# Tile offsets, the order of the up products, and GpSimd's share in a float32r transformer block

## The chip, the core and the metric

The kernel runs on one core of a Trainium2 chip. The metric is the time of one execution on the device, in microseconds, as the median of several runs. The core has TensorE (PE, matmuls), VectorE (DVE), ScalarE (ACT), GpSimd (POOL), a queue engine (SP) and 16 DMA engines. PE's clock has two levels, 1.2 and 2.4 GHz; "granted clock" 1.00 is 2.4 GHz.

## What is computed

One block of a diffusion transformer over 256 latent tokens and 256 context tokens of width 2048, all in float32: adaLN modulation, a mixing sub-layer with windowed attention and a pooling mixer, a squared-ReLU MLP, and a last RMSNorm.

```python
sh_a, sc_a, g_a, sh_m, sc_m, g_m = ada_modulation(c, w_ada, b_ada)      # silu(c) @ w_ada + b_ada, 2048 x 12288
h  = modulate(rms_norm(x, norm_attn_w), sh_a, sc_a)
q, k, v, u = split_projection(h @ w_in)                                 # 2048 x 2560, latent and context
attn = latent_window_attention(rope(q), rope(k), v, kc, vc, attn_sink)
pool = multiscale_pool(u, pool_w, pool_scale)
x  = x + g_a * (concat([attn, pool]) @ w_out)                           # 2048 x 2048
hm = modulate(rms_norm(x, norm_mlp_w), sh_m, sc_m)
x  = x + g_m * (square(relu(hm @ w_up)) @ w_down)                       # 2048 x 8192, 8192 x 2048
return rms_norm(x, final_norm_w)
```

## The kernel before

**Products.** A float32 product is made of float32r products: each operand is split into a high part (a cast on ACT) and a low part (a subtraction), and three matmuls are added in PSUM, high by high, high by low and low by high (`mm3`, lines 280 to 282). A matmul reads a stationary operand (128 columns, loaded by its own instruction, PEld in the profile) and a moving operand (256 or 512 columns).

**Weights.** `WeightStream` brings all weights in order, in tiles of 1 MB through five `raw` slots, on SP's queue. Each half of a weight tile is split by `split_to`: the cast to `hi` on ACT (line 89), the subtraction to `lo` (line 91) on DVE, or, for every third half among the first 140 tiles, on POOL. `hi` and `lo` have six slots each, and the splits run six halves ahead of their use. Tiles of w_ada are used unsplit, on PE (line 297) or, for some columns, on DVE as sums of scaled rows (`ada_v`, line 319).

**Stages.** (1) Up to about 200 us, normalization and the in-projection: `ps_k` and `ps_qu` take the weights as stationary and the activations `hhi`, `hlo` as moving operand, `ps_v` the other way round; w_ada for the attention is spread between them. (2) Attention to about 320 us. (3) The out-projection, `ps_w`: the tiles `mx` stationary, weights moving; after each group of 512 columns, DVE multiplies by the gate, POOL (DVE in the last group) adds the residual (line 817), ACT takes the squares. (4) The first three up groups with `mm3` and the rest of the late w_ada work, to about 525 us. (5) Then 13 up groups and 8 rounds of down products in turn. An up group (`up_group`) keeps four PSUM banks; for each weight tile it walks 4 banks by 4 rows of the tile and issues a wide matmul (`hi` with high and low activations side by side, 512 columns, line 876) and a narrow one (`lo` with the high activations, 256 columns, line 877) in turn. `activation` turns the four sums into `ahi` and `alo`. A down product (`down_group`) has `ahi` and `alo` stationary and the weights moving. The order of the instructions on each engine follows the code.

**Where tiles lie.** A pool puts its tags one after the other in the order in which they are first asked for, each with all its slots; pools on the left side grow upwards, each after the one that is open before it, and those on the right downwards. Every slice that a matmul takes of the tiles named below starts a multiple of 512 bytes into its tile, so the start of an operand modulo 512 is that of its tile. In the built program of the kernel before they start at these bytes of each partition (modulo 512 in brackets): `hi` 64672 (160), `lo` 89248 (160), all `mx` tiles (160), `hhi` and `hlo` in the pool hpa 187872 and 191968 (480), in hpb 130208 and 134304 (160), `ahi` 182048 (288), `alo` 194336 (288). The pool hpa serves the chunks 0, 1, 4 and 5 of the activations, hpb the chunks 2, 3, 6 and 7.

## Time and profile before

| | us |
|---|---|
| median of 3 runs (1172.6 to 1174.21) | 1173.42 |
| the profiled execution, its own time | 1171.78 |
| its span, first to last instruction | 1170.0 |
| PE busy | 1120.1 (96%) |
| DVE busy | 820.6 (70%) |
| ACT busy | 507.4 (43%) |
| POOL busy | 145.2 (12%) |
| mean granted clock | 0.983 |

"Busy" is the time in which an engine executes; matmuls are pipelined, so the time of one of them in a row (0.39 us for 512 columns) is longer than the step from its start to the next one's start. The pace of a product is the step between starts. A group of instructions is shown as line, engine, operation, output<-inputs, shapes and count, then busy time and mean ns of one, then idle time before them and what ended it. Times in a timeline count from the start of the span.

### The profile page before, as it was taken

To read this page: it belongs to the slowest core of one execution; us is meant where nothing else is said; L and a number is where in the kernel's file an instruction comes from. 1 tells how busy PE (TensorE), PEld (TensorE's weight loads), DVE (VectorE), ACT (ScalarE), POOL (GpSimd) and SP (SyncE) were. 2 spreads that over 40 slices of the span, in tenths; PEclk is the share of its full clock that TensorE was granted. 3 is DMA by queue.
4 is the path that set the end of the run, shared out by engine and by line. 5 is a ranking of instruction groups with operands and counts; after the bars stand their busy time and mean duration, and the time that the engine had idled before them with its cause. 6 is when DMAs were issued, how large, how long until landed. Compare 5 with 4: busy or idle time off the path is not lost.

```text
span 1170.0 us, 16111 instructions
## 1 busy us (share of the span) xinstructions
PE 1120.1 (96%) x6308; PEld 905.4 (77%) x6308; DVE 820.6 (70%) x1255; ACT 507.4 (43%) x760; POOL 145.2 (12%) x98
## 2 busy tenths in 40 slices
PE   3999999989999979899999999999999999999996
PEld 2767788746588859888888888888888888888884
DVE  5655467988698888897865775774664664676576
ACT  4633233377543433365433433443533543543452
POOL 1011124610143312330000000000000000000001
PEclk9999999989999979999999999999999999999998
DMA  9999898667898899968785685686556655565531
GB/s 342 331 335 330 287 333 272 224 233 264 272 327 279 294 328 316 329 241 287 254 274 187 232 276 180 235 287 197 181 181 186 200 189 180 190 199 187 180 108 72
DMA packets 174012, 286.64 MB, mean 245 GB/s; under 512 B 5609, under 2 KB 72353, under 8 KB 172785
## 3 DMA queue, kind: packets, MB, share of 16 engines
q1 hardware_dynamic: 172800, 279.55, 71.3%
q0 software_dynamic: 848, 5.55, 1.3%
q8 instruction: 49, 0.80, 0.3%
q10 hardware_dynamic: 288, 0.52, 0.1%
q14 instruction: 27, 0.21, 0.0%
HBM read 283.50 MB, written 2.10 MB: 244 GB/s over the span
## 4 chain that ended last, share of the span: by engine, by line
PE 81%; DVE 11%; DMA 3%; issue 2%; ACT 1%; SPq 1%; DVEq 0%; ACTq 0%
PE ps_up L876 17%; PE ps_d L281 10%; PE ps_d L282 10%; PE ps_d L280 10%; PE ps_up L877 8%; PE ps_ada L297 4%; DVE ada_v L319 3%; DVE lo L91 3%; PE ps_qu L280 2%; PE ps_qu L282 2%; PE ps_qu L281 2%; PE ps_o L725 2%; DMA raw<-in_w_in_dram 1%; PE tp_p L714 1%; PE ps_w L280 1%
## 5 line engine op out<-in xcount | busy, mean ns | idle before, releaser
L91 DVE TENSOR_TENSOR lo<-raw,hi 128x1024 fp32r<-128x1024 f32 x293 | 376.1, 1298 | 212.4 <-ACT hi L89 212.0
L89 ACT CAST hi<-raw 128x1024 fp32r<-128x1024 f32 x330 | 338.0, 1050 | 400.5 <-PE ps_d L282 157.3
L876 PE MATMUL ps_up<-mx,hi 128*128 128x512 f32 x832 | 293.3, 397 | 0.0
L877 PE MATMUL ps_up<-mx,lo 128*128 128x256 f32 x832 | 233.0, 280 | 0.0
L280 PE MATMUL ps_d<-hi,ahi 128*128 128x512 f32 x512 | 200.8, 395 | 0.0
L281 PE MATMUL ps_d<-lo,ahi 128*128 128x512 f32 x512 | 200.7, 395 | 0.0
L282 PE MATMUL ps_d<-hi,alo 128*128 128x512 f32 x512 | 197.8, 395 | 0.0
L876 PEld LDWEIGHTS ps_up<-mx,hi 128*128 128x128 f32 x832 | 156.1, 188 | 37.9 <-issue 1.0
L877 PEld LDWEIGHTS ps_up<-mx,lo 128*128 128x128 f32 x832 | 157.0, 189 | 1.1 <-issue 1.0
L91 POOL TENSOR_TENSOR lo<-raw,hi 128x1024 fp32r<-128x1024 f32 x37 | 95.3, 2577 | 333.1 <-ACT hi L89 304.2
L319 DVE SCALAR_TENSOR_TENSOR ada_v<-raw,c_sil,ada_v 128x512 f32<-128x512 f32 x135 | 124.4, 921 | 13.8 <-DMA raw<-in_w_ada_dram 12.0
L280 PEld LDWEIGHTS ps_d<-hi,ahi 128*128 128x128 f32 x512 | 96.4, 188 | 22.7
L282 PEld LDWEIGHTS ps_d<-hi,alo 128*128 128x128 f32 x512 | 96.4, 188 | 22.7
L281 PEld LDWEIGHTS ps_d<-lo,ahi 128*128 128x128 f32 x512 | 96.4, 188 | 22.4
L280 PE MATMUL ps_qu<-hhi,hi 128*128 128x256 f32 x256 | 75.2, 294 | 5.9 <-ACT hhi L447 5.9
L297 PE MATMUL ps_ada<-raw,c_sil 128*32 128x512 f32 x480 | 73.8, 626 | 0.2 <-DMA raw<-in_w_ada_dram 0.2
L281 PE MATMUL ps_qu<-hlo,hi 128*128 128x256 f32 x256 | 72.4, 284 | 0.0
L282 PE MATMUL ps_qu<-hhi,lo 128*128 128x256 f32 x256 | 71.8, 284 | 0.0
L957 POOL DMA_DIRECT2D fw<-in_final_norm_w_dram x1 | 0.6, 571 | 569.0 <-DVE lo L91 569.0
L280 PEld LDWEIGHTS ps_qu<-hhi,hi 128*128 128x128 f32 x256 | 49.0, 191 | 23.9 <-issue 11.9
L282 PE MATMUL ps_up<-mx,lo 128*128 128x256 f32 x192 | 53.1, 285 | 4.6 <-DVE lo L91 4.6
L281 PE MATMUL ps_up<-mx,hi 128*128 128x256 f32 x192 | 53.7, 283 | 0.0
(196 smaller groups left out, 1457.1 us busy)
## 6 DMA issues: line engine op xcount, KB each, us to landing
raw<-in_w_ada_dram SPq DMA_DIRECT2D x128, 512.0 KB, 7.3
raw<-in_w_mlp_up_dram SPq DMA_DIRECT2D x64, 1024.0 KB, 5.5
raw<-in_w_mlp_down_dram SPq DMA_DIRECT2D x64, 1024.0 KB, 5.1
raw<-in_w_ada_dram SPq DMA_DIRECT2D x32, 1024.0 KB, 6.6
raw<-in_w_in_dram SPq DMA_DIRECT2D x19, 1024.0 KB, 7.0
raw<-in_w_out_dram SPq DMA_DIRECT2D x16, 1024.0 KB, 6.7
xnat<-in_x_dram SPq DMA_DIRECT2D x2, 1024.0 KB, 6.0
xnat<-in_ctx_dram SPq DMA_DIRECT2D x2, 1024.0 KB, 11.8
```

The source lines that it names most:

```text
L89: nc.scalar.copy(hi, raw)
L91: eng.tensor_tensor(lo, raw, hi.bitcast(F32), ALU.subtract)
L280: nc.tensor.matmul(ps, a[0], b[0], start=first, stop=False, skip_group_check=True)
L281: nc.tensor.matmul(ps, a[0], b[1], start=False, stop=False, skip_group_check=True)
L282: nc.tensor.matmul(ps, a[1], b[0], start=False, stop=last, skip_group_check=True)
L297: nc.tensor.matmul(ps[32 * j : 32 * j + 32, :], c_sil[:, 4 * kg + j, :], raw[:, j, :], start=(kg == 0), stop=(kg == 3), tile_position=(0, ...
L319: nc.vector.scalar_tensor_tensor(box["e"], raw[:, j, :], sc, box["e"], ALU.mult, ALU.add)
L714: nc.tensor.transpose(tp[:, P * k : P * k + P], self.p[:, i, P * k : P * k + P], ident)
L725: nc.tensor.matmul(ps[64 * i : 64 * i + 64, 0:T], va[k // 2][:, k % 2, 64 * g : 64 * g + 64], pT[:, k, i, :], start=(k == 0), stop=(k == 3 ...
L876: nc.tensor.matmul(pss[m], hi, hm[k][2], start=k == 0, stop=False, skip_group_check=True)
L877: nc.tensor.matmul(pss[m][:, 0:T], lo, hm[k][0], start=False, stop=k == KC - 1, skip_group_check=True)
L957: nc.gpsimd.dma_start(out=fw, in_=final_w.partition_broadcast(P))
```

## The change

1. Gap tiles, which no instruction reads or writes, move the tiles behind them: 320 bytes between `hi` and `lo`, 192 at the start of mixa and of hpb, 320 between `hhi` and `hlo` (which are now two slots of one tag each), 320 at the end of hpa, 64 between `ahi` and `alo`. `rstd`'s scratch tiles of the last norm (192 bytes) go from the pool mp to yp. From the sizes the starts modulo 512 become:

| tile | before | after |
|---|---|---|
| `hi` | 160 | 160 |
| `lo` | 160 | 480 |
| `mx` | 160 | 160 |
| `hhi`, hpa / hpb | 480 / 160 | 352 / 352 |
| `hlo`, hpa / hpb | 480 / 160 | 160 / 160 |
| `ahi` | 288 | 416 |
| `alo` | 288 | 480 |

(`ahi`: the pool mp ends where x2 starts, at 212960, and holds 2048 + 12288 + 64 + 12288 + 2048 + 4096 bytes, so it starts at 180128 and `ahi` at 182176.) The tiles of the attention's scores do not move.

2. In `up_group` the 16 wide matmuls of a weight tile come first, then its 16 narrow ones.

3. POOL computes no lower parts and no residual additions: 37 subtractions of line 91 and six additions of line 817 go to DVE.

```diff
-POOL_SPLITS = 140
+def gap(pool, n, name="gap"):
+    pool.tile([P, n // 4], F32, tag=name, name=name, bufs=1)
@@ split_to
             hi = self.pool.tile([P, 2, 512], F32R, tag="hi", name="hi", bufs=N_HALF)
+            if not self.n_half:
+                gap(self.pool, 320)
             lo = self.pool.tile([P, 2, 512], F32R, tag="lo", name="lo", bufs=N_HALF)
             nc.scalar.copy(hi, raw)
-            eng = nc.gpsimd if i < POOL_SPLITS and self.n_half % 3 == 1 else nc.vector
-            eng.tensor_tensor(lo, raw, hi.bitcast(F32), ALU.subtract)
+            nc.vector.tensor_tensor(lo, raw, hi.bitcast(F32), ALU.subtract)
@@ modulated
-            hhi = pool.tile([P, 2, 512], F32R, tag=f"hhi{c_ % 2}", name="hhi", bufs=1)
-            hlo = pool.tile([P, 2, 512], F32R, tag=f"hlo{c_ % 2}", name="hlo", bufs=1)
+            hhi = pool.tile([P, 2, 512], F32R, tag="hhi", name="hhi", bufs=2)
+            if c_ in (0, 2):
+                gap(pool, 320, "gaph")
+            hlo = pool.tile([P, 2, 512], F32R, tag="hlo", name="hlo", bufs=2)
@@ where the pools are opened and closed
             mixa = ctx.enter_context(tc.tile_pool(name="mixa", bufs=1, side="left", reuse_waits="tile"))
+            gap(mixa, 192)
             hpb = hpb_es.enter_context(tc.tile_pool(name="hpb", bufs=1, side="left", reuse_waits="tile"))
+            gap(hpb, 192)
+    gap(hpa, 320)
     st_es.close()
     hpa_es.close()
@@ out_group
-            eng = nc.vector if dg == 3 else nc.gpsimd
-            eng.tensor_tensor(xs, xs, t, ALU.add)
+            nc.vector.tensor_tensor(xs, xs, t, ALU.add)
@@ activation
         ahi = mp.tile([P, 4, T], F32R, tag="ahi", name="ahi", bufs=3)
+        gap(mp, 64)
         alo = mp.tile([P, 4, T], F32R, tag="alo", name="alo", bufs=3)
@@ up_group
-            for m in range(4):
-                for j in range(4):
-                    k = 4 * kg + j
-                    hi, lo = w(j, slice(P * m, P * m + P))
-                    nc.tensor.matmul(pss[m], hi, hm[k][2], start=k == 0, stop=False, skip_group_check=True)
-                    nc.tensor.matmul(pss[m][:, 0:T], lo, hm[k][0], start=False, stop=k == KC - 1, skip_group_check=True)
+            for part in range(2):
+                for m in range(4):
+                    for j in range(4):
+                        k = 4 * kg + j
+                        wk = w(j, slice(P * m, P * m + P))[part]
+                        ps, h = (pss[m][:, 0:T], hm[k][0]) if part else (pss[m], hm[k][2])
+                        nc.tensor.matmul(ps, wk, h, start=part == k == 0, stop=part == 1 and k == KC - 1, skip_group_check=True)
@@ finish
-        r = rstd(mp, (ss3[:, i, 3:4], mean[:, i : i + 1]), 1)
+        r = rstd(yp, (ss3[:, i, 3:4], mean[:, i : i + 1]), 1)
```

## Rows read from the trace of the kernel before

**Rows 1.** Stretches: length, busy us of PE PEld DVE ACT POOL, clock, DMA share
```profile
60.00:190.00 130.00, 130.00 (x947) 99.25 (x945) 74.28 (x117) 40.12 (x49) 27.96 (x19) 1.00 0.95 317
190.00:320.00 130.00, 122.16 (x804) 79.25 (x802) 109.01 (x250) 75.97 (x175) 37.73 (x33) 0.96 0.72 248
320.00:390.00 70.00, 70.00 (x329) 57.36 (x328) 61.12 (x60) 27.53 (x35) 27.67 (x13) 1.00 0.91 312
390.00:493.00 103.00, 91.71 (x638) 81.27 (x636) 90.83 (x130) 39.42 (x56) 28.53 (x13) 0.93 0.92 310
493.00:1150.00 657.00, 656.89 (x3282) 551.19 (x3282) 439.87 (x554) 288.57 (x382) 11.81 (x5) 1.00 0.63 209
```

**Rows 2.** Chain of waits from 390 to 493 us, shares by line
```profile
by line: DVE ada_v L319 27.3%; DVE lo L91 20.2%; issue 15.9%; DMA raw<-in_w_out_dram 8.0%; DMA raw<-in_w_mlp_up_dram 5.7%; PE ps_up L282 3.9%; PE ps_up L280 3.4%; PE ps_up L281 3.4%; PE ps_adac L327 2.1%; ACT hi L89 2.1%; DVE mx L848 2.1%; 
```

**Rows 3.** Stretches, one product's matmuls alone: w_out, down, up (PE busy, matmuls)
```profile
329.93:351.27 21.34, 21.34 (x95) 1.00 0.93 314
1023.77:1068.15 44.38, 44.23 (x191) 1.00 0.59 191
979.39:1023.65 44.26, 44.12 (x255) 1.00 0.57 186
```

**Rows 4.** Timeline of PE, v product (start us, us, what); 14 matmuls between
```profile
145.29 0.28 PE L280 MATMUL ps_v<-hi,hhi 128*128 128x256 f32 x1
...
146.99 0.28 PE L280 MATMUL ps_v<-hi,hhi 128*128 128x256 f32 x1
```

**Rows 5.** Timeline of PE, qu product at 213 us; 14 matmuls between
```profile
212.93 0.28 PE L281 MATMUL ps_qu<-hlo,hi 128*128 128x256 f32 x1
...
214.73 0.28 PE L281 MATMUL ps_qu<-hlo,hi 128*128 128x256 f32 x1
```

**Rows 6.** Timeline of PE, qu product at 177 us; 11 matmuls between
```profile
176.68 0.28 PE L280 MATMUL ps_qu<-hhi,hi 128*128 128x256 f32 x1
...
178.09 0.28 PE L280 MATMUL ps_qu<-hhi,hi 128*128 128x256 f32 x1
```

**Rows 7.** Timeline at 700.46 us: a matmul and the next weight load (PEld)
```profile
700.46 0.40 PE L282 MATMUL ps_d<-hi,alo 128*128 128x512 f32 x1
700.46 0.19 PEld L280 LDWEIGHTS ps_d<-hi,ahi 128*128 128x128 f32 x1
```

**Rows 8.** Timeline of PE, k product; 11 matmuls between
```profile
140.21 0.39 PE L280 MATMUL ps_k<-hhi,hi 128*128 128x512 f32 x1
...
142.95 0.39 PE L281 MATMUL ps_k<-hlo,hi 128*128 128x512 f32 x1
```

**Rows 9.** Page, part 5: counts of the narrow up product, a down line
```profile
L877 PE MATMUL ps_up<-mx,lo 128*128 128x256 f32 x832 | 233.0, 280 | 0.0
L280 PE MATMUL ps_d<-hi,ahi 128*128 128x512 f32 x512 | 200.8, 395 | 0.0
```

**Rows 10.** Groups of POOL, 190 to 493 us: busy us, mean ns, idle before
```profile
L91 POOL TENSOR_TENSOR lo<-raw,hi 128x1024 fp32r<-128x1024 f32 x22 | 56.8, 2581 | 160.9 <-ACT hi L89 160.9
L817 POOL TENSOR_TENSOR x<-x,t 128x512 f32<-128x512 f32 x6 | 11.0, 1835 | 10.5 <-DVE t L815 10.5
```

**Rows 11.** Groups of DVE, 570 to 1150 us, where POOL computes nothing
```profile
L91 DVE TENSOR_TENSOR lo<-raw,hi 128x1024 fp32r<-128x1024 f32 x206 | 248.4, 1221 | 164.1 <-ACT hi L89 163.9
L319 DVE SCALAR_TENSOR_TENSOR ada_v<-raw,c_sil,ada_v 128x512 f32<-128x512 f32 x38 | 28.3, 746 | 11.4 <-DMA raw<-in_w_ada_dram 11.2
L861 DVE TENSOR_TENSOR act<-ps_up,act 128x256 f32<-128x256 f32 x52 | 21.6, 419 | 2.5 <-ACT act L860 2.3
L864 DVE TENSOR_TENSOR alo<-act,ahi 128x256 fp32r<-128x256 f32 x52 | 20.4, 420 | 2.6
```

**Rows 12.** Groups of DVE, 190 to 493 us
```profile
L319 DVE SCALAR_TENSOR_TENSOR ada_v<-raw,c_sil,ada_v 128x512 f32<-128x512 f32 x75 | 75.5, 1007 | 1.4
L91 DVE TENSOR_TENSOR lo<-raw,hi 128x1024 fp32r<-128x1024 f32 x42 | 67.4, 1617 | 15.2 <-ACT hi L89 15.2
```

**Rows 13.** Line 817 on DVE: min/median/max ns, first and last start
```profile
L817 DVE TENSOR_TENSOR x<-x,t x2: 691/692/692, 413.3 to 414.6; 128x512 f32<-128x512 f32 x2
```

## The prediction, made before the changed kernel ran

> **What bounds the kernel now.** I read the stretches first [rows 1], because the busy shares of the whole span mix three regimes. From 493 to 1150 us TensorE (PE) is busy 656.89 of 657 us at full clock, while the DMA share is 0.63 and VectorE (DVE) and ScalarE (ACT) are idle a third of the time or more: there only the pace of the matmuls counts, and a nanosecond off each one comes off the end. From 60 to 190 and from 320 to 390 us PE is busy all the time too, with a DMA share of 0.95 and 0.91, so a faster PE gains there only what the transfers leave. From 390 to 493 us PE idles 11.3 us, the clock is 0.93 and DVE is busy 90.8 of 103 us; the chain there goes through DVE by 47% and through "issue", time that no releaser explains, by 16% [rows 2]. From 190 to 320 us PE idles 7.8 us behind the softmax on DVE.
>
> Next I read the pace of the matmuls, start to start, in stretches without a break. At 2.4 GHz a matmul of 512 columns needs 213.3 ns and one of 256 columns 106.7 ns. What stands above that differs by product although the shapes are equal [rows 3]: w_out 21.34 us over 94 steps = 227.1 ns; down 44.38 / 191 = 232.4 ns; a pair of up products (512 and 256 columns) 44.26 over 255 steps, two to a pair, = 347.1 ns. With 256 columns, v at 145 us takes 1.70 us for 15 steps = 113.3 ns [rows 4], qu at 213 us 1.80 / 15 = 120.0 ns [rows 5], qu at 177 us 1.41 / 12 = 117.5 ns [rows 6]. The weight load of the next matmul starts with the running one [rows 7], so what runs together is one matmul's moving operand and the next one's stationary operand. I order the paces by how the start of the moving tile lies to that of the stationary tile, modulo 512 bytes, from the table of offsets above: equal (160 beside 160) costs 13.8 ns over the ideal at 512 columns and 13.3 at 256; +192 (160 beside 480) 6.7 ns; +320 (480 beside 160) 10.8 ns at 256 columns and, for k, 2.74 us / 12 = 228.3 ns, so 15.0 at 512 [rows 8]; -128 (down, 160 beside 288) 19.1 ns. DVE and ACT work beside all of them, so I take the offsets as the cause.
>
> The Trainium skill says the opposite ("TensorE: Matmul & The Clock Gate", Step-by-step: what each phase is for): PE has two independent read ports, and loading the next weights takes nothing from the running matmul. By it the first half of the sum below is zero; it is rival 1.
>
> **The change part by part.** Sums are made against the profiled execution, 1171.8 us (span 1170.0), which lies 1.6 us under the median of 1173.4.
>
> *Up products (832 pairs [rows 9]).* With all 16 wide ones of a tile first, a wide matmul runs beside wide weights (160 beside 160, equal) at the 227.1 ns of w_out; the narrow ones run beside the moved lo (160 beside 480, +192) at the 113.3 ns of v. A pair takes 340.4 instead of 347.1 ns: 6.7 x 832 = **-5.6 us**, all on the path. Bounds: 0 (the wide one keeps a pace that makes up for it) and -6.
>
> *Down products (1536, three lines of 512 [rows 9]).* hi beside ahi becomes 160 beside 416 (-256) for two of three, lo beside alo 480 beside 480 (equal) for the third. The equal one goes to 227.1: 5.3 x 512 = -2.7 us. No row shows -256. Bounds: the cheapest excess, 6.7 ns, gives 220.0, and the dearest, down's own, 232.4; so 1024 of them bring -12.7 to 0 us. I take the equal pace, 227.1, which lies in the middle and is what two of the four offsets come near to: -5.4. Together **-8.1 us**, from -2.7 to -15.4.
>
> *First up groups, in-projection, w_out.* In the first up groups one of three matmuls goes from 120.0 to 113.3, 192 x 6.7 ns = 1.3 us in all, but most of them run before 493 us: **-0.3**. The qu products all become +192 (352 beside 160, 160 beside 480): from 120.0 or 117.5 to 113.3. Of 768 some 480 lie between 60 and 190 us (192 of group 2 from hpb at 120.0, 288 of groups 1 and 3 from hpa at 117.5): -1.3 - 1.2 = **-2.5**, where the DMA at 0.95 follows; half of v loses 4 ns and the other half gains 2.5, which is 0.1. Bounds 0 and -3.5. In w_out one of three goes to +320: 128 x 1.2 ns = **+0.2**.
>
> *GpSimd (POOL) gives its work to DVE.* 22 lower parts of 2.58 us and 6 additions of 1.84 us lie on POOL between 190 and 493 us [rows 10]. They are not free: while one runs, DVE's two-input operations stand. A lower part on DVE takes 1.22 us in the stretch where POOL is idle, an ada_v step 0.746 [rows 11]; between 190 and 493 us they take 1.617 and 1.007 [rows 12]. The excess is 42 x 0.396 + 75 x 0.261 = 36.2 us of DVE. What DVE gets instead is 22 x 1.22 + 6 x 0.69 (as the two additions that it already does [rows 13]) = 31.0 us. So DVE gains 5 us net, and part of the 16% "issue" of [rows 2] (16 us), which falls where POOL operations run, is DVE standing at the same port: I count 6 of it. Against it: a lower part now waits for its cast in DVE's queue, with ada_v, the softmax and the modulation behind it, and those hold the casts' slots and PE. DVE's own lower parts waited 15.2 us for ACT over 42 [rows 12], 0.36 us each; 22 more are 8 us, half of them in time in which DVE idles anyway (42 us of the 303): +4. Net **-7 us**, felt only where PE idles (7.8 + 11.3 us). Bounds +3 and -19. The square on ACT behind each residual addition comes sooner, which is inside this. The 11 lower parts before 190 us and 4 after 493 us add 1.22 us each to a DVE that is busy 57% and 67% there: nothing, or 1 to 2 us if that idle time falls elsewhere.
>
> *Edits that I cost at nothing.* Gap tiles have no instruction. The four sums of an up group now end within the last 1.4 us of it instead of over 5.5; their activations take DVE three operations of 0.42 us each (two of them in [rows 11], the third is as wide), 5.0 us in all, and are needed from 24 down matmuls (5.5 us) after the group on. That cover is thin when lower parts (two per 5.5 us) come between; without it some 1.5 us would be lost at 7 groups, 10 us. hi is freed 1.8 us sooner, which helps the casts. rstd's scratch in another pool and shifted tiles change which old tiles a new one waits for; these readers end long before.
>
> Sum: -5.6 - 8.1 - 0.3 - 2.5 + 0.2 - 7 = -23.3, so 1148.5 for an execution like the profiled one and **1150 us** for the median.
>
> **The rivals.**
> 1. *Offsets do nothing*: the paces differ for another reason (the number of columns per group, what DVE and ACT do). Then only POOL's part stays, -7: **1166**. For it: the loads lie wholly beside running matmuls [rows 7]. The page quoted above speaks for it too. Against it: 113.3 and 120.0 for one shape, and k at w_out's 512 columns and clock is 1.2 ns from it but 4 from down.
> 2. *-256 is as cheap as +192*, and PE's idle time before 493 us shrinks by more: down -15.4 and POOL -12, together -36: **1138**. For it: the lowest excess seen is half of the equal one; nothing shows where it ends.
> 3. *-256 is as dear as down now* and DVE's net is nothing: -5.6 - 2.7 - 2.5 = -11: **1162**.
> 4. *Slower: DVE's queue is held by its casts.* On POOL the 22 lower parts waited 160.9 us for ACT [rows 10], 7.3 us each, and nobody stood behind them. On DVE the softmax, ada_v and modulation do. With 16 us gained by the matmuls and 5 by the port, it turns slower once a lower part holds DVE by more than 1 us on average; at 1.5 us it is +33 - 21: **1185**. Against it: DVE's own hold is 0.36 us, in the same order of casts, and 42 us of DVE idle time take some of it.
>
> **How the numbers follow.** Forecast 0.55 (1143 to 1157), rival 1 0.09, rival 2 0.20, rival 3 0.11, rival 4 0.05. For 8 in 10 the range takes in rival 2 with a little more from DVE and rival 3: 1134 to 1165; most of rival 1 and rival 4 is left out, with the far end of 2. A measurement of this kernel tells about 0.2% from no change, 1171.1 to 1175.8. Faster: the forecast, 2, 3 and nearly all of 1, 0.93; same 0.03; slower 0.04.
>
> **What would show it.** Right: up wide matmuls at 227 and narrow ones at 113 ns; the lo product of down at 227 ns and its two hi products at one other pace; qu at 113 ns throughout; L91 on DVE near 1.22 us and ada_v at 0.75 everywhere, no POOL rows of L91 or L817; PE idle between 390 and 493 us under 8 us. Wrong: down still at 232 ns (rival 3); no pace moved (rival 1); DVE waiting for casts by over 30 us between 190 and 493 us (rival 4); PE gaps at the start of the second half of down groups (activations late).

## The result, and the profile of the changed kernel

| | before | after |
|---|---|---|
| median, us | 1173.01 (1172.51 to 1174.21) | 1162.72 (1161.86 to 1165.18) |
| profiled execution, us | 1171.78 | 1161.86 |
| its span, us | 1170.0 | 1160.1 |
| mean granted clock | 0.983 | 0.983 |

Both medians are of all runs of the comparison. The ratio is 0.9919, with an interval of 0.9904 to 0.9934. The change brings 10.3 us (1173.01 - 1162.72), not 23; the time lies inside the range given, near its upper end. The stretches of the kernel after, in the columns of [rows 1]:

```profile
60.00:190.00 130.00, 130.00 (x936) 98.13 (x935) 74.38 (x121) 39.78 (x48) 3.23 (x7) 1.00 0.96 321
190.00:320.00 130.00, 122.97 (x834) 81.17 (x834) 111.30 (x259) 77.29 (x176) 28.68 (x31) 0.97 0.70 243
320.00:390.00 70.00, 70.00 (x325) 56.49 (x322) 55.78 (x73) 27.17 (x36) 0.76 (x1) 1.00 0.93 323
390.00:493.00 103.00, 96.48 (x679) 86.99 (x678) 87.47 (x146) 39.90 (x57) 0.55 (x1) 0.93 0.99 338
493.00:1150.00 657.00, 655.26 (x3281) 552.77 (x3279) 437.70 (x573) 286.21 (x383) 2.51 (x3) 1.00 0.62 204
```

Against [rows 1], DVE is busy 254.6 us between 190 and 493 us (111.30 + 55.78 + 87.47) where it was 261.0, although it now does the work of 28 POOL operations as well. From 390 to 493 us PE idles 6.5 us instead of 11.3, and the DMA share rose from 0.92 to 0.99. The chain of waits of that stretch has turned over; of the kernel after, from 390 to 493 us, shares by line:

```profile
by line: DMA raw<-in_w_mlp_up_dram 38.1%; DVE lo L99 13.5%; DVE ada_v L327 11.1%; issue 8.5%; ACT hi L98 6.2%; PE ps_ada L305 3.4%; PE ps_up L288 3.2%; PE ps_adac L335 2.5%; PE ps_up L289 1.9%; PE ps_up L290 1.7%; DVE x2T L857 1.2%; PE ps_r
```

In [rows 2] ada_v and the lower parts held 47.5% and the transfers of w_up 5.7%. Now the transfers hold 38.1% and the two DVE lines 24.6%: what is late next is the weights. The reason on DVE's side stands in its groups, kernel after, 190 to 493 us (busy us, mean ns; [rows 12] are the same lines before):

```profile
L99 DVE TENSOR_TENSOR lo<-raw,hi 128x1024 fp32r<-128x1024 f32 x64 | 78.0, 1238 | 18.3 <-ACT hi L98 18.0
L327 DVE SCALAR_TENSOR_TENSOR ada_v<-raw,c_sil,ada_v 128x512 f32<-128x512 f32 x78 | 58.3, 747 | 1.1
```

A lower part fell from 1617 to 1238 ns and an ada_v step from 1007 to 747, as the quiet stretch of [rows 11] had said.

Where the 10 us come from, coarsely, is seen in the first and last start of the down products. The down products of the kernel before, then of the kernel after (first and last start, us):

```profile
L280 PE MATMUL ps_d<-hi,ahi x512: 387/393/404, 506.2 to 1157.7; 128*128 128x512 f32 x171
L282 PE MATMUL ps_d<-hi,alo x512: 389/393/404, 506.7 to 1158.1; 128*128 128x512 f32 x171
```

```profile
L288 PE MATMUL ps_d<-hi,ahi x512: 387/395/401, 501.4 to 1147.4; 128*128 128x512 f32 x171
L290 PE MATMUL ps_d<-hi,alo x512: 387/391/402, 501.8 to 1147.9; 128*128 128x512 f32 x171
```

Everything ahead of the first down product brings 4.8 us (506.2 to 501.4). From there to the last one it is 646.5 us instead of 651.9, so 5.4 us from the eight rounds of down and the 13 up groups between them, where only the pace of PE counts. The forecast had -9.6 and -13.7 for these two parts. That pace, in the kernel after: the last down round (191 steps), the last two up groups (255 steps) and an unbroken stretch of w_out (48 steps), each from the start of its first matmul to that of its last; the count in a row includes one or two more that overlap the edges.

```profile
1103.71:1147.86 44.15, 44.15 (x193) 1.00 0.17 59
1059.41:1103.59 44.18, 44.18 (x257) 1.00 0.58 191
340.30:351.43 11.13, 11.13 (x49) 1.00 1.08 369
```

Down: 44.15 / 191 = 231.2 ns, and 232.4 before [rows 3]. Up: 44.18 / 255 = 173.3 per step, 346.5 a pair, and 347.1 in [rows 3]. w_out: 11.13 / 48 = 231.9, where it had 227.1 [rows 3]. Two products gained little and one lost. Where a mean over the whole trace is given from here on, it is over all steps from one start to the next in which nothing lies between.

| ns per matmul | down, 512 | up, wide | up, narrow | up, pair | w_out, 512 | qu, 256 |
|---|---|---|---|---|---|---|
| before | 232.6 | 233.6 | 116.6 | 350.2 | 227.4 | 118.8 |
| after, forecast | 227.1 | 227.1 | 113.3 | 340.4 | 227.5 | 113.3 |
| after, measured | 231.3 | 228.3 | 117.9 | 346.2 | 231.9 | 118.4 |

### The profile page after: what moved, and what is told of

It is laid out like the page before. It is cut to its first block, busy times and chain, and to the rows that moved or that the text cites. A ratio compares the mean times of both kernels' runs of the same rounds, so it can differ in the third digit from the quotient of the medians.

```text
span 1160.1 us, 16052 instructions
## 1 busy us (share of the span) xinstructions
PE 1115.3 (96%) x6308; PEld 904.8 (78%) x6308; DVE 803.4 (69%) x1298; ACT 503.6 (43%) x760; POOL 40.4 (3%) x55
## 4 chain that ended last, share of the span: by engine, by line
PE 81%; DVE 9%; DMA 6%; ACT 2%; issue 1%; SPq 1%; DVEq 0%; ACTq 0%
PE ps_up L894 25%; PE ps_d L288 10%; PE ps_d L289 10%; PE ps_d L290 10%; PE ps_ada L305 5%; DMA raw<-in_w_mlp_up_dram 3%; DVE lo L99 3%; PE ps_qu L288 2%; PE ps_qu L289 2%; PE ps_qu L290 2%; PE ps_o L738 2%; DMA raw<-in_w_in_dram 2%; DVE ada_v L327 1%; PE tp_p L727 1%; PE ps_w L288 1%
## 5 line engine op out<-in xcount | busy, mean ns | idle before, releaser
L99 DVE TENSOR_TENSOR lo<-raw,hi 128x1024 fp32r<-128x1024 f32 x330 | 396.8, 1224 | 223.1 <-ACT hi L98 216.1
L894 PE MATMUL ps_up<-mx,hi 128*128 128x512 f32 x832 | 200.0, 392 | 0.0
L894 PEld LDWEIGHTS ps_up<-mx,hi 128*128 128x128 f32 x832 | 153.4, 188 | 31.8 <-issue 1.9
L327 DVE SCALAR_TENSOR_TENSOR ada_v<-raw,c_sil,ada_v 128x512 f32<-128x512 f32 x135 | 100.8, 747 | 18.3 <-DMA raw<-in_w_ada_dram 16.8
L894 PEld LDWEIGHTS ps_up<-mx,lo 128*128 128x128 f32 x832 | 105.3, 189 | 4.0
L894 PE MATMUL ps_up<-mx,lo 128*128 128x256 f32 x832 | 106.6, 281 | 0.0
L288 PE MATMUL ps_up<-mx,hi 128*128 128x256 f32 x192 | 54.4, 292 | 1.5 <-ACT mx L859 1.5
L289 PE MATMUL ps_up<-mx,hi 128*128 128x256 f32 x192 | 54.1, 286 | 0.0
L290 PE MATMUL ps_up<-mx,lo 128*128 128x256 f32 x192 | 53.0, 287 | 0.1
L290 PEld LDWEIGHTS ps_qu<-hhi,lo 128*128 128x128 f32 x256 | 48.9, 192 | 3.4 <-issue 1.7
```

Of the source, the lines that this page charges most:

```text
L99: nc.vector.tensor_tensor(lo, raw, hi.bitcast(F32), ALU.subtract)
L288: nc.tensor.matmul(ps, a[0], b[0], start=first, stop=False, skip_group_check=True)
L289: nc.tensor.matmul(ps, a[0], b[1], start=False, stop=False, skip_group_check=True)
L290: nc.tensor.matmul(ps, a[1], b[0], start=False, stop=last, skip_group_check=True)
L327: nc.vector.scalar_tensor_tensor(box["e"], raw[:, j, :], sc, box["e"], ALU.mult, ALU.add)
L894: nc.tensor.matmul(ps, wk, h, start=part == k == 0, stop=part == 1 and k == KC - 1, skip_group_check=True)
```

## The experiments

Two questions were open: which part of the change brings what, and why the paces don't follow the offsets as the forecast had them. The times:

| kernel | median, us | before, in the same comparison | ratio to before, interval |
|---|---|---|---|
| e_gaps | 1168.30 | 1172.56 | 0.9945 [0.9925, 0.9966] |
| e_order | 1169.91 | 1172.56 | 0.9967 [0.9952, 0.9982] |
| e_pool | 1166.10 | 1172.56 | 0.9924 [0.9900, 0.9947] |
| e_pool15 | 1163.66 | 1173.06 | 0.9921 [0.9897, 0.9945] |
| e_down | 1163.36 | 1173.06 | 0.9914 [0.9893, 0.9935] |
| e_mix | 1166.84 | 1172.71 | 0.9943 [0.9921, 0.9964] |
| e_mod256 | 1164.13 | 1172.71 | 0.9931 [0.9911, 0.9950] |
| v_best | 1155.29 | 1173.06 | 0.9851 [0.9825, 0.9878] |
| v_best2 | 1156.03 | 1172.71 | 0.9858 [0.9833, 0.9882] |

Ratio and interval stand as they are on record. For the first three the quotient of the two medians is nearer to 1 (0.9964, 0.9977 and 0.9945), though inside the interval, so their gains are known to some 2 us only. Each trace is of one execution of its kernel.

### e_gaps, e_order, e_pool: each part of the change alone

e_gaps is the kernel before with the gap tiles and the moved scratch:

```diff
+            if not self.n_half:
+                gap(self.pool, 320)
...
+            if c_ in (0, 2):
+                gap(pool, 320, "gaph")
...
+            gap(mixa, 192)
...
+            gap(hpb, 192)
...
+    gap(hpa, 320)
...
+        gap(mp, 64)
...
-        r = rstd(mp, (ss3[:, i, 3:4], mean[:, i : i + 1]), 1)
+        r = rstd(yp, (ss3[:, i, 3:4], mean[:, i : i + 1]), 1)
```

> The kernel before with the gap tiles and the moved scratch alone (order of the up products and GpSimd's work as before). Theory A, the recorded one (the pace of a matmul follows from how its moving operand lies to the next stationary operand modulo 512 bytes, whatever its neighbours do): down loses 8.1 us, the in-projection 2.5, so about 1162 us. Theory B (a product settles into a rhythm of loads and matmuls; offsets give a fast pace only when all its matmuls have the same relation, and a product that mixes relations falls out of it): down gains the 1.8 us that the trace of the changed kernel shows, w_out loses 1.5, so 1171 to 1175 us, no change that can be told.

Measured: 1168.30. Down runs at 231.6 ns, an up pair at 346.7, qu at 118.4, w_out at 231.9. By the medians all offsets together bring 4.3 us (1172.56 - 1168.30), a time that neither theory had: A lies 6.3 us under it, B 2.7 us or more above. The paces of down, qu and w_out are those of theory B; what B left out are the up products, 832 x (350.2 - 346.7) = 2.9 us. In the trace, of an execution of 1170.10 us, the first down product starts at 508.8 us, 2.6 later than in the kernel before, and the way from there to the last one is 647.7 us instead of 651.9.

e_order has the wide products of a weight tile first, and nothing else of the change:

```diff
+            for part in range(2):
+                for m in range(4):
+                    for j in range(4):
+                        wk = w(j, slice(P * m, P * m + P))[part]
...
```

> The kernel before with the up products' order alone: 16 wide matmuls of a tile first, then 16 narrow ones, all operands at 160 modulo 512. Both theories: a wide one at 227.1 ns as in w_out, a narrow one at 120.0 ns as in the first up groups, together the 347.1 ns that a pair takes now, so 1173 us, no change. If it is faster by 2 us or more, the order itself is worth something and the gaps less.

Measured: 1169.91. Wide 228.4, narrow 119.5, pair 347.9 instead of 350.2; 832 x 2.3 = 1.9 us, and the way from the first down product to the last (506.7 to 1156.3 us) is 649.6 us instead of 651.9. So the order alone lowers the wide ones by 5 ns and raises the narrow ones by 3. Both paces are near the 227.1 and 120.0 that were expected; what the expectation had wrong is the pair of the kernel before, 350.2 and not 347.1. Gaps alone give a pair of 346.7, the order alone 347.9, and both together, in the kernel after, 346.2: they do not add up.

e_pool moves POOL's lower parts and additions to DVE:

```diff
-            eng = nc.gpsimd if i < POOL_SPLITS and self.n_half % 3 == 1 else nc.vector
-            eng.tensor_tensor(lo, raw, hi.bitcast(F32), ALU.subtract)
+            nc.vector.tensor_tensor(lo, raw, hi.bitcast(F32), ALU.subtract)
...
-            eng = nc.vector if dg == 3 else nc.gpsimd
-            eng.tensor_tensor(xs, xs, t, ALU.add)
+            nc.vector.tensor_tensor(xs, xs, t, ALU.add)
```

> The kernel before with GpSimd's lower parts and residual additions on VectorE alone. Theory A: 7 us less, 1166 us. Theory C (VectorE gains its time, but in the stretch from 390 to 510 us the transfers then end last, so part of it is given back): the first down product starts about 5 us earlier, 1168 us. If the 3 us that the changed kernel loses before 108 us come from the lower parts that VectorE took over and not from the gaps, they show here as well.

Measured: 1166.10, the time of theory A, with the earlier start and the late transfers of theory C. The down products of e_pool (first and last start) and its chain of waits from 390 to 493 us by line:

```profile
L279 PE MATMUL ps_d<-hi,ahi x512: 387/393/404, 500.8 to 1152.2; 128*128 128x512 f32 x171
L281 PE MATMUL ps_d<-hi,alo x512: 389/393/404, 501.2 to 1152.7; 128*128 128x512 f32 x171
```

```profile
by line: DMA raw<-in_w_mlp_up_dram 22.9%; PE ps_up L279 12.4%; PE ps_up L280 11.3%; PE ps_up L281 11.2%; DVE ada_v L318 9.7%; DVE lo L90 6.0%; issue 5.4%; PE ps_ada L296 4.7%; PE ps_adac L326 4.0%; ACT hi L89 3.1%; DVE x2T L843 1.2%; PE ps_
```

All of its gain lies ahead of the first down product: 506.2 to 500.8 is 5.4 us, and from there to the end both kernels take 651.9 us. ada_v, lower parts and "issue" held 63.4% of the chain in [rows 2] and hold 21.1% here.

### e_pool15: POOL keeps its share of the first 15 halves

e_pool was 2.8 us late at the end of the in-projection although it ends early. The last k products of the kernel before, of e_pool and of e_pool15 (first and last start):

```profile
L281 PE MATMUL ps_k<-hlo,hi x32: 387/390/501, 54.3 to 186.6; 128*128 128x512 f32 x32
```

```profile
L280 PE MATMUL ps_k<-hlo,hi x32: 387/392/501, 55.8 to 189.4; 128*128 128x512 f32 x32
```

```profile
L281 PE MATMUL ps_k<-hlo,hi x32: 387/392/503, 54.4 to 186.9; 128*128 128x512 f32 x32
```

The third is this kernel, which is e_pool but for the five lower parts among the first 15 halves, which POOL keeps:

```diff
-            eng = nc.gpsimd if i < POOL_SPLITS and self.n_half % 3 == 1 else nc.vector
+            eng = nc.gpsimd if self.n_half < 15 and self.n_half % 3 == 1 else nc.vector
...
-            eng = nc.vector if dg == 3 else nc.gpsimd
-            eng.tensor_tensor(xs, xs, t, ALU.add)
+            nc.vector.tensor_tensor(xs, xs, t, ALU.add)
```

> GpSimd's work on VectorE as in the run e_pool, but the first five of its lower parts (every third of the first 15 halves, to about 110 us) stay on GpSimd. If the 2.8 us that e_pool loses before 108 us come from those lower parts, this one is at the time of before at the second chunk pair and 2.8 us under e_pool in the end, 1163 us. If they come from something else (the clock's return after the first transposes), the loss stays.

Measured: 1163.66, as expected; the interval of its ratio is nearly that of e_pool, so the time doesn't tell the two apart, but the trace does: the last k product starts at 186.9 us, 0.3 us from the kernel before. Part of the loss is made from 24 to 40 us. That stretch in the kernel before and in e_pool (columns of [rows 1]; e_pool15 has 67 matmuls at 0.79 there, as the kernel before):

```profile
24.00:40.00 16.00, 10.08 (x67) 7.61 (x67) 12.46 (x46) 7.14 (x15) 2.42 (x1) 0.79 1.06 372
```

```profile
24.00:40.00 16.00, 9.92 (x56) 7.00 (x60) 11.28 (x47) 7.21 (x16) 0.00 (x0) 0.68 1.06 373
```

PE idles some 6 of these 16 us in each. With no POOL work the granted clock is 0.68 instead of 0.79, that is, PE is longer at 1.2 GHz, and 56 matmuls are done instead of 67. Which wait of the first halves makes the difference was not followed further. The first down product of e_pool15 starts earlier still, 10.3 us before that of the kernel before, in an execution of 1161.49 us, 2.2 under the median:

```profile
L280 PE MATMUL ps_d<-hi,ahi x512: 387/393/405, 495.9 to 1147.4; 128*128 128x512 f32 x171
```

### m_offsets: rows of matmuls by the difference of their starts

A kernel that holds only rows of matmuls on one tile and computes nothing of the block. In a row all moving operands start at 160 modulo 512 and all stationary ones d bytes below that, for 16 values of d, 512 and 256 columns wide, once with d rising and once falling; then come the patterns of offsets of the kernels before and after.

```diff
+def uniform(name, width, d, n):
+    return (name, [(width, 2048 * (k % 4) + 160, 17408 + 512 * (k % 8) + 160 - d) for k in range(n)])
```

> A measuring kernel: it computes nothing of the block (the output is a copy of a few sums), only rows of matmuls at chosen offsets, 512 and 256 columns wide, in one stretch on TensorE. First each difference between moving and stationary operand from 0 to 480 bytes in steps of 32, the same for all matmuls of a row, once upwards and once downwards; then the patterns of the products as they lie in the kernel before and after. Theory A: the pace depends on the difference alone, the same in both directions: 227 ns at 0, 232 at -128, 120 and 113 ns at 0 and +192 with 256 columns; down after at 227 on average. Theory B: the uniform rows agree with that, but the mixed patterns do not follow from them: down after near 231, w_out after near 232, qu after near 118.

Measured, in stretches of this kernel from the start of one matmul to that of a later one. First four rows of 512 columns with d = 0, 32, 64 and 160 (23 steps each), then four of 256 columns with d = 0, 192, 448 and, falling, 192 (32 steps each):

```profile
503.59:508.81 5.22, 5.22 (x25) 1.00 0.00 0
495.28:500.65 5.37, 5.37 (x25) 1.00 0.00 0
486.99:492.25 5.26, 5.26 (x24) 1.00 0.00 0
64.62:70.01 5.39, 5.39 (x24) 1.00 0.01 3
155.67:159.51 3.84, 3.84 (x35) 1.00 0.02 4
189.69:193.31 3.62, 3.62 (x34) 1.00 0.00 0
234.93:238.55 3.62, 3.62 (x34) 1.00 0.00 0
561.88:565.64 3.76, 3.76 (x34) 1.00 0.00 0
```

512 columns: 5.22 / 23 = 227.0 ns, then 233.5, 228.7 and 234.3. 256 columns: 3.84 / 32 = 120.0, then 113.1, 113.1 and 117.5. DVE, ACT and the DMA engines do next to nothing here, so the offset alone moves the pace. That the start of the moving operand counts as well is seen in qu before: the stationary operands start at 160 in both pools, and with the moving ones at 160 a step takes 120.0 ns [rows 5], with those at 480 it takes 117.5 [rows 6]; the rows of the same differences modulo 256 (0 and 64) take 120.0 and 117.8. Three things come out that the forecast had not. The 512-column rows for d and d + 256 agree within the measurement over all 16 values, so the period is 256 bytes and not 512; the differences other than 0 and 64 take 232.5 to 234.3 ns. What is cheapest for 512 columns (0) is among the dearest for 256. And the same d = 192 runs at 113.1 in one place and 117.5 in another: with 256 columns there are two rhythms, and the offsets of a row do not decide which one it falls into. What ran before it is a likely cause that no run isolates.

Then the patterns, high, low, high as in `mm3`: down before, down after, w_out after, qu after, v before (hpa), v after (47 steps each), and the up pairs before (32 steps):

```profile
249.92:260.85 10.93, 10.93 (x49) 1.00 0.00 0
266.63:277.49 10.86, 10.86 (x48) 1.00 0.01 2
283.30:294.20 10.90, 10.90 (x48) 1.00 0.00 0
330.74:336.31 5.57, 5.57 (x50) 1.00 0.00 0
339.15:344.47 5.32, 5.32 (x49) 1.00 0.01 3
347.40:352.94 5.54, 5.54 (x49) 1.00 0.00 0
364.25:369.91 5.66, 5.66 (x34) 1.00 0.00 0
```

That is 232.6, 231.1, 231.9, 118.5, 113.2, 117.9 and 176.9 per step: each within 1 ns of what the same product does in the kernels (232.6, 231.3, 231.9, 118.4, [rows 4] 113.3, 117.7, and 176.8 in the slower of the up groups before). The sequence of starts thus gives the paces without any work on DVE, ACT or the DMA engines beside it, except for which of the two rhythms a row takes. The mixed patterns of the kernel after are what spoils them: 231.1 for down, although modulo 256 each moving operand starts where the stationary operand of the next matmul does (hi where ahi does, lo where alo does).

### m_patterns: which operands must agree

Again rows of matmuls alone, now with operands that alternate between two starts.

```diff
+pattern("own" + o, 512, (A, B), (A, B))       # moving = own stationary, next differs
+pattern("nxt" + o, 512, (B, A), (A, B))       # moving = next stationary, own differs
...
+pattern("base", 512, (A,), (A,))
```

> A second measuring kernel, which computes nothing of the block: rows of matmuls on TensorE. First two offsets A = 160 and B = A + 64, + 128 or + 32 in turn, as moving, stationary or both. If only a matmul's moving operand against the next stationary one counts (the recorded reading), the rows in which these two are equal run at 226.7 ns and the rows in which a matmul's own two are equal do not. If the own pair counts it is the other way round; if the whole sequence counts, neither is at 226.7. Then down with lo 64 beyond hi modulo 256 and 8 by 8 offsets of ahi and alo: by theory B none of the 64 reaches 226.7. Then up groups, 16 wide at relation 0 and 16 narrow, four times, at eight relations of the narrow ones: with +192 the narrow ones run at 113.3 as the uniform row did, or at the 117.8 of the changed kernel, if what stands in front of a row decides which of two rhythms it takes.

Measured for starts 64 bytes apart: moving equal to its own stationary operand (21 steps), moving equal to the next one's, and all equal (23 steps each). The first row is PE's first work in this kernel, and its first steps take 427 ns, that is 512 columns at 1.2 GHz, although the clock column has 1.00 there; the stretch begins behind them.

```profile
24.60:29.46 4.86, 4.86 (x22) 1.00 0.00 0
32.47:37.80 5.33, 5.33 (x24) 1.00 0.00 0
140.74:145.95 5.21, 5.21 (x24) 1.00 0.00 0
```

231.4, 231.7 and 226.5 ns. The forecast had paired each moving operand with the stationary one that is loaded beside it, which is the second row: it should have run at 227 and takes 231.7. Pairing with its own operand does no better. So neither pair sets the pace, the third of the outcomes named above. Of 64 patterns of down with lo moved by 64 bytes, and ahi and alo at each of eight starts, none came under 228.6 ns. In blocks of 16 wide and 16 narrow matmuls the narrow ones take 117.3 to 120.5 ns at every offset tried, not 113. The least time per matmul, at 512 columns, came from a sequence with one relation throughout.

### e_down, e_mix, e_mod256: the same in the kernel

By that, down needs hi, lo, ahi and alo at one start modulo 256 and no gap at lo. e_down is the kernel before with rstd's scratch moved and 64 bytes behind alo, which puts ahi and alo to 160 modulo 256, where hi and lo are:

```diff
         alo = mp.tile([P, 4, T], F32R, tag="alo", name="alo", bufs=3)
+        mp.tile([P, 16], F32, tag="gap", name="gap", bufs=1)
...
-        r = rstd(mp, (ss3[:, i, 3:4], mean[:, i : i + 1]), 1)
+        r = rstd(yp, (ss3[:, i, 3:4], mean[:, i : i + 1]), 1)
```

> The kernel before with one shift alone: the last norm's scratch goes to the pool yp and 64 unused bytes stand behind alo, so that ahi and alo start at 160 modulo 256, as hi and lo do. Theory B (a product has its fast rhythm only when all its matmuls have one and the same relation, and that relation counts modulo 256): down goes from 232.4 to 226.7 ns, 1536 x 5.7 = -8.8 us, nothing else moves: 1164 us. Theory A' (the recorded one, modulo 256 instead of 512, each matmul for itself): the same here, but by it the changed kernel's down, which has the relation 0 modulo 256 in all three of its matmuls, would have had this pace too. A rival: neighbours on other engines, and not offsets, set down's pace: 232 ns and 1173 us.

e_mix has the same 64 bytes one line further up, so that alo alone starts at 224:

```diff
         ahi = mp.tile([P, 4, T], F32R, tag="ahi", name="ahi", bufs=3)
+        mp.tile([P, 16], F32, tag="gap", name="gap", bufs=1)
         alo = mp.tile([P, 4, T], F32R, tag="alo", name="alo", bufs=3)
```

> The run e_down with its 64 unused bytes in front of alo instead of behind it, as the change has them: ahi at 160, alo at 224 modulo 256, hi and lo at 160 both. Theory B: one of three stationary operands with another relation takes the whole product out of its rhythm: down near 232 ns again, the 8.8 us are gone, 1171 to 1173 us. Theory A' (each matmul for itself): the two matmuls beside ahi keep 226.7 ns, so at most a third of the gain is lost, 1166 us.

e_mod256 is e_down with 256 bytes more in front of lo and in front of alo (lo, mx and alo move by 256):

```diff
+                self.pool.tile([P, 64], F32, tag="gap", name="gap", bufs=1)
...
+        mp.tile([P, 64], F32, tag="gap256", name="gap256", bufs=1)
         alo = mp.tile([P, 4, T], F32R, tag="alo", name="alo", bufs=3)
```

> The run e_down with lo, the mx tiles and alo 256 bytes further on: hi 160, lo 416, ahi 160, alo 416 modulo 512, all 160 modulo 256. If the relation counts modulo 256, every pace is that of e_down (down 226.9, w_out 227.4, first up groups 119.9 ns) and the time 1163 us. If it counts modulo 512, down mixes relations of 0 and 256 and falls back to about 232 ns, 1172 us, and w_out to 232 ns.

The last down round (191 steps) and the last two up groups (255 steps) of e_down, of e_mix and of e_mod256:

```profile
1105.96:1149.32 43.36, 43.36 (x194) 1.00 0.18 64
1060.75:1105.85 45.10, 45.10 (x257) 1.00 0.57 185
```

```profile
1111.79:1155.92 44.13, 44.13 (x193) 1.00 0.18 64
1067.41:1111.67 44.26, 44.26 (x256) 1.00 0.57 186
```

```profile
1106.63:1149.99 43.36, 43.36 (x194) 1.00 0.18 63
1061.42:1106.51 45.09, 45.09 (x257) 1.00 0.55 185
```

| modulo 256 | hi | lo | ahi | alo | down, last round | median, us |
|---|---|---|---|---|---|---|
| before | 160 | 160 | 32 | 32 | 232.4 | 1173.01 |
| after | 160 | 224 | 160 | 224 | 231.2 | 1162.72 |
| e_down | 160 | 160 | 160 | 160 | 227.0 | 1163.36 |
| e_mix | 160 | 160 | 160 | 224 | 231.0 | 1166.84 |
| e_mod256 | 160 | 160 | 160 | 160 | 227.0 | 1164.13 |

One operand of four that is 64 bytes off takes back 4.0 of the 5.4 ns; 256 bytes on two of them change nothing. e_down alone, by one gap of 64 bytes and the moved scratch, is as fast as the whole change. e_down and e_mod256 came out as expected. The time of e_mix did not: 1166.84 is 4 us under theory B's, near that of A', while its down pace is theory B's. The difference lies in its up groups, which take 346.7 ns a pair, 832 x 3.5 = 2.9 us less than in the kernel before.

These up groups show the two rhythms again. Their code and their operands are the same in e_down and e_mix, and in the first four of the seven stretches of up groups they have the same pace. In the last three, two groups take 45.10 us in e_down and 44.26 in e_mix: a down round of e_down gains 0.77 us against e_mix (44.13 - 43.36), and the up groups behind it lose 0.84. The pace of the round before them is not what decides in general, since in the kernel before up groups of 173.6 and of 176.8 ns per step both follow rounds of 232.3 to 232.4 ns.

### v_best and v_best2: what the findings make together

v_best is e_pool, e_order and e_down in one: no gap but the one behind alo.

```diff
-            eng = nc.gpsimd if i < POOL_SPLITS and self.n_half % 3 == 1 else nc.vector
-            eng.tensor_tensor(lo, raw, hi.bitcast(F32), ALU.subtract)
+            nc.vector.tensor_tensor(lo, raw, hi.bitcast(F32), ALU.subtract)
...
-            eng = nc.vector if dg == 3 else nc.gpsimd
-            eng.tensor_tensor(xs, xs, t, ALU.add)
+            nc.vector.tensor_tensor(xs, xs, t, ALU.add)
...
+        mp.tile([P, 16], F32, tag="gap", name="gap", bufs=1)
...
+            for part in range(2):
...
-        r = rstd(mp, (ss3[:, i, 3:4], mean[:, i : i + 1]), 1)
+        r = rstd(yp, (ss3[:, i, 3:4], mean[:, i : i + 1]), 1)
```

> What the experiments point to: the kernel before with GpSimd's lower parts and additions on VectorE, the up products' order, and ahi and alo at 160 modulo 256; none of the other gaps. Sum of the parts measured so far in the ledgers of the stages: VectorE -5.4, order -2.3, down -8.8 us: 1156 us. If offsets matter only through the mix of relations, w_out stays at 227.3 ns and up at 228 and 119.5 ns.

v_best2 also leaves POOL its share of the first 15 halves, as e_pool15.

> The run v_best with the first five of GpSimd's lower parts kept on GpSimd, as in e_pool15. v_best came out at 1155.3 us and lost 2.0 us before 108 us against the kernel before; e_pool15 lost 0.3 there. So 1153 us, if the parts add up.

Measured: 1155.29, where 1156 was expected, and 1156.03, where 1153 was. v_best beats both kernels: 17.8 us under before (1173.06 in its runs). The down products of v_best (first and last start), then its last down round and last two up groups:

```profile
L279 PE MATMUL ps_d<-hi,ahi x512: 389/389/396, 500.2 to 1140.8; 128*128 128x512 f32 x171
L281 PE MATMUL ps_d<-hi,alo x512: 388/389/396, 500.7 to 1141.3; 128*128 128x512 f32 x171
```

```profile
1097.97:1141.29 43.32, 43.32 (x194) 1.00 0.17 60
1053.46:1097.85 44.39, 44.39 (x257) 1.00 0.58 193
```

6.0 us lie ahead of the first down product (506.2 to 500.2) and 10.8 behind it (641.1 us instead of 651.9): 1536 x (232.6 - 226.8) = 8.9 of down and 832 x (350.2 - 347.8) = 2.0 of up. With the wide products first the last up groups, behind a fast down round, take 44.39 us instead of the 45.10 of e_down. v_best2 gains nothing more: its last k product starts at 187.3 us, where v_best's does at 188.7, and by the starts of its matmuls it is 8.4 us ahead of the kernel before at 477 us, but 4.7 of them are gone at 502 us. In v_best2 PE idles 4.0 of the 10 us from 480 to 490 us, at a granted clock of 0.76, and in v_best 2.1 us at 1.00; why the wait is longer was not followed.

## Why the prediction was right or wrong

**Down, -8.1: wrong, measured 1536 x (232.6 - 231.3) = -2.0.** The step that failed is "what runs together is one matmul's moving operand and the next one's stationary operand", and with it pricing each matmul of a product by the pace of a uniform row. In a uniform row the value taken for -256 was even right: e_down has that relation everywhere and runs at 227.0, the 227.1 of the text. But the change also moves lo, and with it alo, by 64 bytes modulo 256; m_offsets gives 231.1 for that mixture, and in m_patterns the agreement of each moving operand with the next stationary one gives 231.7 ns and not 227. The bounds, -2.7 to -15.4, were made of uniform paces too, and the result lies just outside.

**Up, -5.6: wrong, measured 832 x (350.2 - 346.2) = -3.3.** The wide ones came to 228.3, near the 227.1 taken from w_out, but the narrow ones to 117.9 instead of v's 113.3: v in hpa was in the faster of two rhythms, and no block behind wide matmuls was seen in it. On the other side the 347.1 of [rows 3] was too low for the start: it holds for two of the last three stretches of up products, the third runs at 176.8 per step, 353.6 a pair, and the mean of all is 350.2. One row had been read for all.

**qu -2.5 and w_out +0.2: wrong.** qu went from 118.8 to 118.4 ns. In w_out, a product in which all operands had one start (160), the moved lo gives one matmul of three another relation, and 227.4 became 231.9: 384 x 4.5 = +1.7 us. It had been booked as 1.2 ns on one matmul in three; it is the clearest sign that the cost does not stay with the matmul that is moved. All stationary operands of w_out start at 160, so its matmuls have the relations 0 and 64 modulo 256 whichever pair is taken, the own or the next; the uniform rows of these take 227.0 and 228.7 ns, and the mixture takes more than either. The k products, which the sum leaves out, went from 229.2 to 233.0 ns, 96 x 3.8 = +0.4 us.

**POOL to DVE, -7: right in its mechanism; by the start of the first down product -5.4 in e_pool and -10.3 in e_pool15.** The excess on DVE's operations went as worked out (lower part 1238 ns, ada_v 747), DVE gained 6.4 us between 190 and 493 us where 5 were forecast, and "issue" fell by half. Two things hold e_pool under the forecast. The lower parts before 190 us were costed at nothing or 1 to 2 us and cost 2.8, which e_pool15 takes back. And the gain of 390 to 480 us was not all kept: transfers end last there. The stretch from 480 to 490 us in the kernel after, in the kernel before and in e_pool15 (columns of [rows 1]):

```profile
480.00:490.00 10.00, 7.68 (x47) 7.22 (x46) 8.24 (x15) 1.85 (x3) 0.00 (x0) 0.74 1.04 389
```

```profile
480.00:490.00 10.00, 9.77 (x80) 9.60 (x80) 9.96 (x9) 4.56 (x5) 5.12 (x2) 1.00 0.83 287
```

```profile
480.00:490.00 10.00, 8.16 (x67) 8.10 (x68) 6.37 (x15) 3.20 (x8) 0.00 (x0) 1.00 0.99 351
```

PE idles 2.3 of 10 us in the kernel after, the DMA share is 1.04, and the granted clock is 0.74. In e_pool it idles 2.4 us at 0.85, in e_pool15 1.8 us at full clock, with 67 matmuls done instead of 50: part of the gain seems to hang on whether the clock falls in this wait, though these are single executions. The last quarter of the first three up groups starts 7.5 us sooner than in the kernel before (485 us there), in the kernel after and in e_pool alike; at their end it is 4.8 and 5.4. The prediction said that a faster PE gains before 390 us only what the transfers leave; it did not carry that to 390 to 493 us, where DVE's relief puts the transfers last.

**The rivals.** Rival 1, that offsets do nothing, is refuted: a gap of 64 bytes and the moved scratch are worth 9.7 us (e_down, 1173.06 - 1163.36), and m_offsets shows 227.0 to 234.3 ns by the offset alone. The Trainium skill ("TensorE: Matmul & The Clock Gate", Step-by-step: what each phase is for) has the loading of the next weights take nothing from the running matmul. The measurement does not fit that: in uniform rows the start of the stationary operand alone moves the pace by up to 7.3 ns a matmul, though no run shows where the two operands meet. Rival 3 had nearly the right time, 1162, with another story: its -256 as dear as down before is contradicted by e_down, and its "nothing" for DVE by e_pool. Rival 2 is contradicted by the 227.0 as well. Rival 4, DVE's queue held by its casts, did not come: the waits of the kernel after from 190 to 493 us (total us, times, longest):

```profile
ACT hi L98 <- DMA raw<-in_w_mlp_up_dram: 33.3, 12, 4.7
ACT hi L98 <- DMA raw<-in_w_out_dram: 27.6, 8, 6.6
DVE lo L99 <- ACT hi L98: 18.0, 16, 3.8
```

DVE waits 18.0 us for casts, 2.8 more than in [rows 12] and under the 30 that were named as its sign. The casts themselves wait for transfers. Nor did the four sums of an up group that end together cost anything: PE of the kernel after is busy for all 654.00 us from 493 to 1147 us, so no down product waits for its activations.

**The sum.** Behind the first down product -13.7 was forecast and -5.4 came, which is down and up; ahead of it -9.6 against -4.8, which is qu, w_out, the first halves and the transfers at 480 us. The range held because it had been opened to the dear end of the unknown offset: it held by luck, since -256 turned out cheap and the gain was lost to the mixture, for which the sum has no term.

**What stays open.** Why the period is 256 bytes, and which part of the chip two operands meet in, no run tells; nor what decides between 113 and 118 ns, so that v's faster rhythm could not be brought into the up groups. No rule gives the pace of a mixture from its starts. Alignments of hhi and hlo that give qu the relation 192 throughout, 113.1 ns in a uniform row, were not tried.

## What to carry to other kernels

A pace read from a product in which all operands have one relation holds for such a product only; before moving a tile, write the sequence of starts of moving and stationary operands with the real order of the matmuls, and look for the arrangement in which all have one relation, for 512 columns that of equal starts (here 64 bytes in one place and a moved scratch were worth as much as six gaps, a new order and the move of POOL's work together). Read a pace from all groups of a product and not from one, since the same code can run in two rhythms. And when work is taken off the engine that ends last, name the next to end last in that very stretch, here the weight transfers, before counting the whole gain.

## What the runs showed of the hardware

- The pace of float32r matmuls of 512 columns depends on the starts of the operands in their partitions, modulo 256 bytes: 227.0 ns with equal starts, 228.7 with the moving one 64 bytes above, 232.5 to 234.3 at the others tried (m_offsets, steps of 32 bytes; 227.0 again with 256 bytes more on two of the four tiles, e_mod256). With 256 columns equal starts are among the dearest, 120.0.
- Sequences of mixed starts have paces of their own, which the uniform paces of their members don't give: w_out after mixes relations of 227.0 and 228.7 ns and takes 231.9.
- With 256 columns the same starts run at 113 or at 118 ns (m_offsets, d = 192), and up groups with the same code and operands at 173.6 or 176.8 ns per step (e_mix and e_down, last three rounds). Whole up groups stay in one of the two; what decides is not known.
